# The first stage of a decoder step: pages of the cache in halves by two queues, x and w_ada asked for later, PSUM pools that wait by tile, and the last pair's compression sums without a pin

## The chip, the core and the metric

One core of a Trainium2 chip runs the whole program. Its engines are PE (TensorE, matrix products), DVE (VectorE), ACT (ScalarE), POOL (GpSimd) and SP (SyncE, which here only issues DMAs). Each engine works off its own queue of instructions in a fixed order; semaphores hold an instruction back until what it reads or overwrites is ready. DMAs are issued by SP, POOL and ACT, and an issue stands in the queue of its engine like any other instruction.

The metric is the device time in microseconds (us) of one execution, as the median of several runs.

## The reference, cut to what matters

One layer of a decoder runs over 512 prompt tokens and over 8 sampled sequences with 8 new tokens each and 2048 tokens in a paged cache. The part that matters here is the compression of the cached keys and values, and the normalization ahead of the first projection:

```python
def compress_blocks(x, pos, w1, w2):
    b, n = x.shape[:2]
    n_chunk = n // CMP_STRIDE
    xc = x[:, :n_chunk * CMP_STRIDE].reshape(b, n_chunk, CMP_STRIDE, NSA_GROUPS, HEAD_DIM)
    pos = pos.reshape(2, CMP_STRIDE, 1, HEAD_DIM)
    w1 = w1.reshape(2, CMP_STRIDE, HEAD_DIM, CMP_HIDDEN)
    lead = jnp.einsum('bncgd,cdh->bngh', xc + pos[0], w1[0])
    trail = jnp.einsum('bncgd,cdh->bngh', xc + pos[1], w1[1])
    return jnp.einsum('bngh,hd->bngd', jax.nn.silu(lead[:, :-1] + trail[:, 1:]), w2)
...
    mod = jnp.einsum('bd,de->be', jax.nn.silu(c), lp['w_ada']) + lp['b_ada']
    sh1, sc1, gt1, sh2, sc2, gt2 = jnp.split(mod[:, None, :], 6, axis=-1)
    h = rms_norm(x, lp['norm1_g']) * (1.0 + sc1) + sh1
    z = jnp.einsum('btd,dc->btc', h, lp['w_in'])
```

Everything after that (two attention branches, gates, output projection, MLP) is untouched.

## The kernel before

The program has stages: the first stage (`first_stage`, L542), the projection `z` in eight slabs (`step` in `run`, L2583, and `project`, L873), prompt attention, sample attention, the merge of the branches, and the MLP. Only the first stage and its seam with the projection are touched.

**Units.** The first stage compresses the pages of 8 sequences in 48 units (L578). Sequences 0 to 3 have 8 units each: four steps j, each once for keys (kv = 0) and once for values (kv = 1). Sequences 4 and 5 share 8 units, and 6 and 7 the last 8. Two sequences make a pair, and a pair adds up in three PSUM banks: `hid` for keys, `hid` for values, and one, `hids`, that both share. For every unit PE turns rows of a page (`ct` in the trace), ACT copies them out (`x`), DVE or, for the shared units, POOL makes their sums (`xs`), and PE multiplies them by the weights w1 (`hid`, then `hids`). The order on PE is: `ct` of unit u+1, `hid` and `hids` of unit u, then what the list `todo[u]` holds. `ro` is a copy on DVE that brings the page of a sequence (`cpg`, four buffers) into the order of the transposes.

**Sums.** When a pair is done, `cmp_act` (L503) reads its banks on ACT and DVE once for keys and once for values (in the trace `cst` and `csx`, and `r1w` for the last pair), and leaves silu of the sums; `cmp_out` multiplies that by w2. For pairs 0 to 2 it stands in `todo[14]`, `todo[15]` and so on; for pair 3 it comes after the loop, behind a pin (L678 to L681): its instructions go after the last split on DVE and the last high part on ACT. Keys and values use one buffer, `csx`, which the squares of the norms use too (`norm`, L556).

**Loads.** Pages are asked for by number, so a register is loaded for each; SP asks for half of sequence 0, half of 1, all of 2, then 4 to 7 when a buffer comes free; ACT asks for the other half of 0; POOL asks for the other half of 1 and all of 3 (L621), then w2, the tiles of `x` (three buffers), and eight tiles of `w_ada` (two buffers, 1 MB each), each waiting for the buffer it takes over. Late in that queue stand `late_loads` (L273): ptT, a copy of the page table, and four small constants. `stage_logf` (L696) turns ptT into row numbers (`lfrow`, on DVE) for a gather by POOL. Each DMA is pinned behind the one before it on its queue. `asked(f)` (L613) puts a small copy on POOL ahead of f, which waits for a sum xs.

**x and w_ada.** `norm(k)` takes the squares of x tile k on ACT, a reciprocal root in 13 small operations and a scaling on DVE; `turned(k)` transposes it on PE (`nt`) and copies it to `hf` (`adw` in the trace). `ada_first` (PE, `ada`) and its end make the modulation, and `modulate` applies it to `hf` on DVE.

**The seam.** At unit 46 `seam()` (L2537) opens the pools of the projection, splits the 8 rows of `hf` into high and low parts (`h`, ACT and DVE), and splits the first weights (`winh`, `winl`). The projection's matmuls need both. The first stage's banks come from the pool `psc`: three matmul banks, two for transposes, two for `hid`, one for `hids`. Then the pool `ps` takes the same eight banks (L2564). A pool waits, by default, for all of the pool before it; with `reuse_waits="tile"` a tile waits for the tiles whose place it takes. SBUF pools have that (L64), PSUM pools do not (L67).

**Order.** The order within each queue is made when the kernel is built, by a scheduler with a simulated time line; among what is ready it goes by the order in which the program is traced. On PE every matmul is chained behind the last one until the first slab of the projection is done, so there the written order holds. `issue_after` pins an instruction behind another one of the same engine.

## Time and profile before

| | |
|---|---|
| median of 3 runs | 1175.04 us (1172.7 to 1177.06) |
| the profiled execution | 1173.28 us, its span 1170.8 us |
| granted TensorE clock, mean | 0.992 |
| busy: PE, DVE, ACT, POOL | 96%, 67%, 48%, 26% |
| read from HBM, written | 217.64 MB, 57.12 MB |

Unit 0 starts on PE at 18.6 us of the span, unit 16 at 54.2, unit 32 at 93.7, unit 47 at 167.0, and the projection at 179.8. Times in the text are us from the start of the span. A row of the timeline gives start, duration, engine, line, operation, output and input with shapes, a count, and in brackets the idle time before it and what ended it. A row of the waits gives the engine, its operation and line, what released it, and then total us, number and longest. A row of the chain of waits gives start, duration, engine, output, line and count. A line number can be that of a helper (L83 is any matmul, L89 any transpose, L106 any tensor-tensor operation of DVE, L168 any DMA).

### The profile page before, as it was taken

What the parts mean: (1) busy time and instruction counts of PE and PEld (TensorE: products, weight loads), DVE (VectorE), ACT (ScalarE), POOL (GpSimd) and SP (SyncE); (2) the same over time, 40 slices, a digit from 0 to 9 for tenths busy, and PEclk for the clock granted to TensorE, in tenths of its full rate; (3) what the DMA queues carried; (4) which work ended last, traced back from release to release, by engine and by line L of the source; (5) the groups of instructions that cost most, each with busy time, mean ns of one, the idle gap of its engine ahead of it and who ended that gap; (6) DMA issues with size and microseconds to landing.
All of it is one profiled execution on the core that took longest, in us unless ns stands there. A gap on an engine that the chain in (4) does not pass through costs nothing.

```text
span 1170.8 us, 25266 instructions
## 1 busy us (share of the span) xinstructions
PE 1129.6 (96%) x9530; PEld 972.4 (83%) x9530; DVE 782.2 (67%) x1874; ACT 564.2 (48%) x1079; POOL 300.1 (26%) x353
## 2 busy tenths in 40 slices
PE   8897988999999998999999999999999999999998
PEld 5896768999865665777799999789999997888887
DVE  3566574668677897766656364768766754798676
ACT  1343352345576785555533222447565655565420
POOL 4314420000220111000576664010655411100000
PEclk9999998999999999999999999999999999999999
DMA  9998535587586559999899997337444537977732
GB/s 231 230 248 228 164 104 192 166 297 257 162 295 216 158 193 314 296 308 305 242 274 299 318 279 252 117 114 235 148 146 154 182 109 251 312 258 250 240 104 81
DMA packets 188187, 255.51 MB, mean 218 GB/s; under 512 B 23161, under 2 KB 144706, under 8 KB 185890
## 3 DMA queue, kind: packets, MB, share of 16 engines
q1 hardware_dynamic: 148770, 173.03, 47.9%
q0 software_dynamic: 21296, 67.38, 17.8%
q10 hardware_dynamic: 18000, 13.50, 4.0%
q8 instruction: 75, 1.23, 0.4%
q14 instruction: 46, 0.38, 0.1%
HBM read 217.64 MB, written 57.12 MB: 235 GB/s over the span
## 4 chain that ended last, share of the span: by engine, by line
PE 83%; DVE 8%; DMA 5%; issue 1%; ACT 1%; SPq 1%; POOL 0%; ACTq 0%; DVEq 0%
PE dn L83 14%; PE z L83 10%; PE mg L83 9%; PE br L83 4%; PE wo L83 4%; PE up L83 3%; DMA cpg<-in_cache_nsa_kv 3%; PE hid L83 3%; PE k L89 2%; PE ss L83 2%; PE so L83 2%; PE dns L83 2%; PE ct L89 2%; PE ada L83 2%; PE hids L83 2%
## 5 line engine op out<-in xcount | busy, mean ns | idle before, releaser
L83 PE MATMUL z<-winh,h 128*128 128x264 f32 (+1 forms) x576 | 111.5, 288 | 10.0 <-DVE r1w L106 10.0
L83 PEld LDWEIGHTS z<-winh,h 128*128 128x128 f32 x576 | 92.6, 193 | 11.5 <-issue 10.9
L83 PE MATMUL z<-winl,h 128*128 128x264 f32 (+1 forms) x320 | 88.7, 286 | 0.0
L83 PE MATMUL mg<-hH,wmh 128*128 128x288 f32 x240 | 70.2, 294 | 0.0
L83 PE MATMUL mg<-hH,wml 128*128 128x288 f32 x240 | 70.1, 294 | 0.0
L83 PE MATMUL mg<-hL,wmh 128*128 128x288 f32 x240 | 68.0, 293 | 0.0
L118 ACT ACTIVATE x<-ct 128x512 f32<-128x512 f32 x64 | 36.4, 596 | 65.4 <-PE ct L89 63.0
L83 PE MATMUL hid<-x,w1raw 128*128 128x128 f32 (+1 forms) x384 | 65.1, 313 | 0.2 <-ACT x L118 0.2
L83 PEld LDWEIGHTS z<-winl,h 128*128 128x128 f32 x320 | 61.3, 192 | 0.1
L83 PEld LDWEIGHTS hid<-x,w1raw 128*128 128x128 f32 x384 | 55.1, 194 | 3.0 <-ACT x L118 0.5
L83 PE MATMUL hids<-xs,w1sum 128*128 128x128 f32 (+1 forms) x192 | 37.7, 320 | 10.2 <-DVE ntt L106 6.0
L137 DVE TENSOR_TENSOR wml<-wmr,wmh 128x1024 fp32r<-128x1024 f32 x14 | 21.2, 1511 | 36.4 <-ACT wmh L118 36.4
L83 PEld LDWEIGHTS mg<-hH,wmh 128*128 128x128 f32 x240 | 45.1, 188 | 0.1
L83 PEld LDWEIGHTS mg<-hH,wml 128*128 128x128 f32 x240 | 45.0, 187 | 0.0
L137 DVE TENSOR_TENSOR wp<-sums,wp 128x1024 fp32r<-128x1024 f32 x26 | 38.3, 1477 | 9.2 <-ACT wp L118 8.7
L83 PEld LDWEIGHTS mg<-hL,wmh 128*128 128x128 f32 x240 | 44.3, 188 | 0.0
L137 DVE TENSOR_TENSOR wp<-pu,wp 128x512 fp32r<-128x512 f32 (+1 forms) x26 | 28.9, 1116 | 18.7 <-ACT wp L118 18.7
L83 PEld LDWEIGHTS hids<-xs,w1sum 128*128 128x128 f32 x192 | 29.9, 197 | 12.8 <-issue 8.6
L2073 POOL TENSOR_TENSOR td<-td 128x512 f32<-128x512 f32 x24 | 34.3, 1429 | 21.0 <-DMA td<-in_w_down 20.9
L89 PE MATMUL ct<-identF,ro 128*128 128x128 f32 x256 | 36.8, 278 | 2.6 <-DVE ro L121 2.6
L2073 POOL TENSOR_TENSOR td<-td,td 128x512 f32<-128x512 f32 x24 | 34.3, 1430 | 14.8 <-DMA td<-in_w_down 14.1
L83 PE MATMUL br<-oH,wbl 128*128 128x288 f32 x128 | 37.8, 295 | 0.0
(1175 smaller groups left out, 3565.6 us busy)
## 6 DMA issues: line engine op xcount, KB each, us to landing
adw<-in_w_ada SPq DMA_DIRECT2D x16, 1024.0 KB
foxD<-in_cache_fox_kv SPq DMA_DIRECT2D x128, 128.0 KB
rows<-in_cache_nsa_kv SPq DMA_DIRECT2D x128, 128.0 KB
rows<-foxD SPq DMA_DIRECT2D x26, 512.0 KB
pu<-in_w_up SPq DMA_DIRECT2D x26, 512.0 KB
wdr<-in_w_down SPq DMA_DIRECT2D x26, 512.0 KB
cpg<-in_cache_nsa_kv SPq DMA_DIRECT2D x96, 128.0 KB
td<-in_w_down POOLq DMA_DIRECT2D x24, 512.0 KB, 6.5
```

Of the source, the lines that this page charges most:

```text
L83: ins = self.nc.tensor.matmul(out, a, b, start=start, stop=stop, skip_group_check=True)
L89: ins = self.nc.tensor.transpose(out, in_, self.identF[:n, :n])
L118: return self.nc.scalar.activation(out, in_, f, **kw)
L137: self.splits.append((eng or self.nc.vector).tensor_tensor(l, x, h.bitcast(F32), op=OP.subtract).ins)
L2073: self.nc.gpsimd.tensor_tensor(out, x, y, op=OP.subtract)
```

## The change

1. PSUM pools get `reuse_waits="tile"`.
2. Of sequences 1, 2 and 3, SP asks for the first half of the pages and POOL for the second, in the order 1, 2, 3.
3. `late_loads` goes from unit 31 to unit 20. The tiles of x are asked for at units 22, 23, 23, 32 and 34 (were 15, 16, 16, 23 and 27), the first two of w_ada at 25 and 27 (24 and 28), the other six one unit later.
4. The norms go to units 29, 31, 33, 34 and 36 (were 18, 22, 26, 30 and 33), the turns to 31, 33, 35, 36 and 38 (22, 26, 30, 33 and 35). `ada_first` goes one unit back for the first six (30, 32, ... 40), the last two stay at 41 and 43. The first two `modulate` go from units 36 and 37 to unit 39. The first `stage_logf` goes from 32 to 33.
5. `cmp_act` of pair 3 is traced in units 46 (keys) and 47 (values), without the pin. Its buffers lie in the tile of w1 (its unused fifth and taps whose last use is unit 46); the tile `r1w` that takes the place of w1 is made after the last pair's keys are out, inside the first slab of the projection.

```diff
     def banks(self, name, ctx, mm):
-        self.ps = ctx.enter_context(self.tc.tile_pool(name=name, bufs=1, space=bass.MemoryType.PSUM))
+        self.ps = ctx.enter_context(self.tc.tile_pool(name=name, bufs=1, space=bass.MemoryType.PSUM, reuse_waits="tile"))
...
-        r1 = self.keep.tile([P, 5 * D], F32, tag="r1", bufs=1, name="w1raw")
+        r1 = self.r1 = self.keep.tile([P, 5 * D], F32, tag="r1", bufs=1, name="w1raw")
...
-        r = self.r1[:, TOK:TOK + 1536].rearrange("p (n c) -> p n c", n=3) if i == 3 else None
-        xb, th = (r[:, 0], r[:, 1 + kv]) if i == 3 else (pl.tile([P, 512], F32, tag="csx", name=f"csx{i}{kv}"),
+        v = self.r1.rearrange("p (n c) -> p n c", c=512)
+        xb, th = (v[:, 8], v[:, 0 if kv else 9]) if i == 3 else (pl.tile([P, 512], F32, tag="csx", name=f"csx{i}{kv}"),
...
-            r = self.r1[:, TOK + 1536:TOK + 2048].rearrange("p (n g d) -> p n g d", n=2, d=64) if i == 3 else None
+            r = self.r1[:, 512:1024].rearrange("p (n g d) -> p n g d", n=2, d=64) if i == 3 else None
...
-        self.cmp_pages("sync", 1, slice(0, 8))
+        for b in (1, 2, 3):
+            self.cmp_pages("sync", b, slice(0, 8))
         self.late_constants()
         self.ada_start()
         self.constants()
-        self.cmp_pages("sync", 2)
...
-        for k, u in enumerate((22, 26, 30, 33, 35)):
-            todo[u - (4 if u < 32 else 3 if u == 33 else 2)] += [lambda k=k: norm(k)]
+        for k, u in enumerate((31, 33, 35, 36, 38)):
+            todo[u - 2] += [lambda k=k: norm(k)]
             todo[u] += [lambda k=k: turned(k)]
...
-        todo[0] += [asked(lambda: (self.cmp_pages("gpsimd", 1, slice(8, 16)), self.cmp_pages("gpsimd", 3)))]
+        todo[0] += [asked(lambda: [self.cmp_pages("gpsimd", b, slice(8, 16)) for b in (1, 2, 3)])]
...
-        todo[15] += [asked(load_x)]
-        todo[16] += [load_x, load_x]
-        todo[24] += [asked(wada(0))]
-        todo[23] += [load_x]
-        todo[27] += [load_x]
-        todo[28] += [asked(wada(1))]
-        todo[31] += [self.late_loads]
+        todo[22] += [asked(load_x)]
+        todo[23] += [load_x, load_x]
+        todo[25] += [asked(wada(0))]
+        todo[32] += [load_x]
+        todo[34] += [load_x]
+        todo[27] += [asked(wada(1))]
+        todo[20] += [self.late_loads]
...
-        for k, u in enumerate((29, 31, 33, 35, 37, 39, 41, 43)):
+        for k, u in enumerate((30, 32, 34, 36, 38, 40, 41, 43)):
...
-                todo[(30, 32, 34, 36, 38, 40)[k - 2]] += [wada(k)]
+                todo[(31, 33, 35, 37, 39, 41)[k - 2]] += [wada(k)]
             if k % 2:
-                todo[max(u + 2, 36)] += [lambda k=k: self.modulate(0, hf, range(k - 1, k + 1))]
+                todo[max(u + 2, 39)] += [lambda k=k: self.modulate(0, hf, range(k - 1, k + 1))]
...
-        for y, u in enumerate((32, 36)):
+        for y, u in enumerate((33, 36)):
...
-        self.r1 = self.keep.tile([P, 5 * D], F32, tag="r1", bufs=1, name="r1w")
-        with behind():
-            for kv in range(2):
-                self.cmp_act(pl, 3, kv)
+            if u >= 46:
+                self.cmp_act(pl, 3, u - 46)
...
-        self.zS = self.r1[:NS, 0:TOK]
+        def room():
+            self.r1 = keep.tile([P, 5 * D], F32, tag="r1", bufs=1, name="r1w")
+            self.zS = self.r1[:NS, 0:TOK]
...
-            step(0, between=[lambda: None] + [lambda kv=kv: self.cmp_out(None, 3, kv) for kv in range(2)] + [lambda: self.cmp_keys(3)])
+            step(0, between=[lambda: None] + [lambda kv=kv: self.cmp_out(None, 3, kv) for kv in range(2)] + [lambda: (self.cmp_keys(3), room())])
```

## The prediction

> **What bounds the kernel now.** I read the page's busy shares first, then the waits of PE (TensorE), then stretches of the span, and the timeline at each wait.

> ```profile
> PE 1129.6 (96%) x9530; PEld 972.4 (83%) x9530; DVE 782.2 (67%) x1874; ACT 564.2 (48%) x1079; POOL 300.1 (26%) x353
> ...
> PE z L83 <- DVE r1w L106: 10.0, 1, 10.0
> PE hids L83 <- DVE ntt L106: 6.0, 1, 6.0
> PE hids L83 <- DVE csx L106: 4.2, 3, 2.1
> ```

> PE is the bound, idle for 41 us of 1170.8. 20.2 of these are the three waits above (us in total, times, longest), and all lie in the first stage, which is what the change rewrites. Whatever is saved there moves everything behind it, since the later stages are PE work with little idle time of their own (325 to 440 us below: PE 110.94 of 115). Of each stretch the rows give its length and the busy time of PE, weight loads, DVE (VectorE), ACT (ScalarE) and POOL (GpSimd), then PE's granted clock, the share of the DMA engines' time, and GB/s.

> ```profile
> 17.00:90.00 73.00, 68.79 (x650) 66.88 (x651) 45.62 (x148) 30.65 (x55) 24.73 (x44) 0.98 0.97 244
> 83.30:110.00 26.70, 20.18 (x162) 16.48 (x161) 15.36 (x56) 10.52 (x20) 10.19 (x12) 0.94 0.99 258
> 110.00:120.00 10.00, 9.30 (x72) 7.72 (x70) 9.27 (x32) 2.99 (x7) 3.77 (x3) 1.00 0.33 107
> 110.00:140.60 30.60, 29.90 (x215) 24.97 (x214) 21.97 (x64) 11.21 (x23) 13.24 (x11) 1.00 0.52 161
> 169.80:180.00 10.20, 0.23 (x1) 0.27 (x2) 8.99 (x20) 4.35 (x8) 1.80 (x5) 0.64 0.87 278
> 325.00:440.00 115.00, 110.94 (x812) 70.96 (x812) 93.61 (x325) 84.39 (x230) 19.94 (x31) 1.00 0.66 214
> ```

> PE stands still almost wholly from 169.8 to 180, with its granted clock down to 0.64, and loses 6.5 us from 83.3 to 110.

> **Part 1, pages in halves.** Before, sequence 2 came by SP alone while POOL fetched sequence 3, which is used a whole sequence later.

> ```profile
> 20.65 4.87 POOL L168 DMA_DIRECT2D cpg<-in_cache_nsa_kv  x8 [0.96 <-issue]
> ...
> 30.34 2.05 POOL L168 DMA_DIRECT2D cpg<-in_cache_nsa_kv  x3 [0.48 <-DMA cpg<-in_cache_nsa_kv]
> ...
> DMA to landing us min/median/max: 4.1/7.0/9.7
> ...
> 49.21 1.90 DVE L121 COPY ro<-cpg 128x1024 f32<-128x1024 f32 x3 [0.92 <-DMA cpg<-in_cache_nsa_kv]
> ...
> 53.24 0.71 PE L83 MATMUL hids<-xs,w1sum 128*128 128x128 f32 x4 [1.60 <-DVE csx L106]
> ...
> 57.35 0.68 PE L83 MATMUL hids<-xs,w1sum 128*128 128x128 f32 x4 [2.06 <-DVE csx L106]
> ```

> The two POOL rows are the first and the last of its first 16 page requests, the last out by 32.4 us. Those 16 are now halves of sequences 1 and 2, so with the longest landing, 9.7 us, sequence 2 is there by 42 us, not 49.2. DVE then loses the 0.92 us ahead of its copy, and the whole row of copies and sums behind it, which PE's two waits follow, comes 0.9 us earlier. The waits themselves stay but for that: DVE works without a gap in between. From nothing to both waits (3.7 us), I take **0.9**: the copy's idle time is the only one that the pages explain. [...] The row from 17 to 90 agrees that the engines are full (0.97); what changes is whose bytes go first.

> **Part 2, the page-table load ahead of x and w_ada.** The 5 small loads with ptT now follow w2 in POOL's queue.

> ```profile
> 52.73 0.18 POOL L616 COPY warm<-xs 128x1 f32<-128x1 f32 x1 [10.28 <-DVE xs L483]
> ...
> 87.00 0.56 POOL L168 DMA_DIRECT2D ptT<-in_page_table  x1
> ...
> 97.04 0.21 DVE L112 TENSOR_SCALAR lfrow<-ptT 128x1 int32<-128x1 int32 x2 [4.94 <-DMA ptT<-in_page_table]
> ...
> 101.56 2.05 PE L83 MATMUL hids<-xs,w1sum 128*128 128x256 f32 x4 [5.98 <-DVE ntt L106]
> ...
> 106.70 1.03 PE L83 MATMUL hids<-xs,w1sum 128*128 128x256 f32 x4
> ```

> They fit into POOL's 10.28 us of idle time, so they cost nothing; ptT is there long before its use, and the 4.94 us in which lfrow held DVE's queue go. Behind lfrow stood the sums that PE's hids waits for. The stretch from 83.3 to 140.6 (unit 29 to unit 40) has 57.3 us with 50.1 of PE, so 7.2 idle; the same four hids also took 2.05 us against 1.03, at a lowered clock: 8.2 in all.

> Against it: the norms of x tiles 0 to 2 and the turns of tiles 0 and 1 move into this stretch.

> ```profile
> L106 DVE TENSOR_TENSOR ntt<-nrs x10: 146/152/162, 64.0 to 110.2; 128x1 f32<-128x1 f32 x8, 64x1 f32<-64x1 f32 x2
> ...
> L110 DVE TENSOR_SCALAR x<-x,nrs x5: 745/753/754, 65.7 to 113.2; 128x1024 f32<-128x1024 f32 x4, 64x1024 f32<-64x1024 f32 x1
> ...
> 70.60 0.87 PE nt L89 x8
> ...
> 88.68 0.68 DVE L121 COPY adw<-nt 128x512 f32<-128x512 f32 x1
> ```

> A norm is 13 small operations of 0.152 and a scaling of 0.753, 2.7 us; a turn is 0.87 of PE and leaves DVE one copy of 0.68. Three norms and two copies are 9.6. DVE had 15.36 + 21.97 = 37.3 in the stretch and gets 46.9. How densely can DVE be filled without PE waiting? Of the rows above the fullest long stretch is 325 to 440 us, 0.81; the fullest short one is 110 to 120, 0.93, with PE at 9.30. PE's own work there becomes 50.1 + 1.7 = 51.8. DVE at 0.93 needs 50.4 us, less than that: no new waits. At 0.81 it needs 57.9: 6.1 us of them. The new stretch is packed like the short one but is long like the other, so I take the middle, **3 us of new waits** (the modulates of units 36 and 37 now meet in unit 39, but stay inside the stretch). Part 2 nets 8.2 - 3 = **5.2**, from 2.1 to 8.2.

> Loads that move cost nothing if these hold:

> ```profile
> x<-in_x_prompt POOLq DMA_DIRECT2D x4, 512.0 KB, 4.6
> wada<-in_w_ada POOLq DMA_DIRECT2D x8, 1024.0 KB, 8.6
> ...
> 130.59 1.73 PE hid L83 x8
> ...
> 142.58 1.73 PE hid L83 x8
> ```

> The last two rows are units 38 and 41, so three units take 12 us. The last two w_ada tiles have three units between the buffer's release and their use (four before); 8.6 us fit. x tile 3 now stands in POOL's queue behind a w_ada tile that waits for unit 30; its norm comes two units, 8 us, after its request; 4.6 fit. POOL's sums xs of the pairs stand behind both, as they did.

> **Part 3, the seam at 170 us.** A PSUM pool that waits as a whole made z's first matmul wait until the last of the old banks was read, at 179.6.

> ```profile
> 168.76 1.03 PE L83 MATMUL hids<-xs,w1sum 128*128 128x256 f32 x4
> ...
> 171.49 2.42 DVE L137 TENSOR_TENSOR winl<-winr,winh 128x1056 fp32r<-128x1056 f32 x2
> 173.83 0.60 DVE L106 TENSOR_TENSOR r1w<-r1w,hid 128x192 f32<-128x192 f32 x3
> 174.34 0.46 DVE L115 SCALAR_TENSOR_TENSOR r1w<-r1w,cmpb,hid 128x256 f32<-128x256 f32 x1
> 174.73 1.24 DVE L137 TENSOR_TENSOR winl<-winr,winh 128x1056 fp32r<-128x1056 f32 x1
> 175.90 0.60 DVE L106 TENSOR_TENSOR r1w<-hids,r1w 128x256 f32<-128x256 f32 x1
> ...
> 179.00 0.61 DVE L106 TENSOR_TENSOR r1w<-hids,r1w 128x256 f32<-128x256 f32 x1
> ...
> 179.76 7.47 PE z L83 x48
> 188.07 2.96 PE z L83 x24
> ```

> With waits by tile, z's first bank (one of the matmul banks, not of the sums) is free at once, and z waits for its operands: the rows of h, and the second half of the first weights, split when the first of the two winl at 171.49 ends (172.7). But a new wait comes: the sums of the last pair's keys are now traced ahead of unit 47, and as in unit 15 (the hids row at 53.24) the hids matmuls of unit 47 must then wait until DVE has read the shared hids bank for the keys. Queued behind these four matmuls is all of z. If DVE does the splits first and the sums at once after them, the read ends at 172.7 + 0.60 + 0.46 + 0.60 = 174.4, hids ends at 175.4, and z starts there, 4.4 us earlier. The idle time is still over 5 us, so z's slow start (7.47 against 2 x 2.96, 1.55 us) stays. [...]

> Ends: with DVE taking the sums before the last splits, half of z's first tile (1.48) is done when they end at 174.4, so it ends at 175.9 at full clock, against 179.76 + 1.55 + 2.96 = 184.3: 8.4. With the next slab's splits ahead too, as at 174.73, the read ends at 176.5: 2.2. I take **4.4**, the order in which these rows stand.

> **Sum.** 0.9 + 5.2 + 4.4 = 10.5. The profiled run took 1173.28 (span 1170.8), so 1162.8; the median, 1175.04, is 1.8 higher: **1164.5**.

> **Rivals.** (a) All of it goes well: DVE at 0.93 and sums before splits, 0.9 + 8.2 + 8.4 = 17.5, 1157.5. For it: the 0.93 of 110 to 120; against: at the seam the rows stand in the other order. (b) DVE becomes the bound of the stretch and the seam gets its low end: 0.9 + 2.1 + 2.2 = 5.2, 1169.8. (c) The change does not do what it says at the seam, because z's first bank lies on one that the sums still read: part 3 pays nothing, 1168.9. The profile does not show which bank is whose. (d) Slower: each turn of x on PE waits for its norm, two units (8 us) after it.

> ```profile
> 86.90 1.05 ACT L118 ACTIVATE sq<-x 128x1024 bf16<-128x1024 f32 x1
> ...
> 101.86 0.75 DVE L110 TENSOR_SCALAR x<-x,nrs 128x1024 f32<-128x1024 f32 x1
> ```

> This norm took 15.7 us, ptT's 4.94 included; the squares also share one buffer with the pair's sums, which now alternate with them. From 10.1 us a norm on (five turns late by 2.1) the 10.5 are gone; at 15.7, three turns late by 7.7, the kernel ends at 1164.5 + 23.1 = 1187.6. Against it: half of the 15.7 is the wait for ptT and what it held up. (e) The halves bring nothing, because the engines are as full with one order as with the other and the copy still waits: 9.6, 1165.4.

> **How the numbers follow.** Forecast 0.46 (own range 1160 to 1168), (e) 0.10, (a) 0.19, (b) 0.13, (c) 0.06, (d) 0.06. A measurement of this kernel tells about 0.5%, 5.9 us, from no change. Faster: the forecast, (e), (a) and a third of (c), 0.77; same: (b), at 5.2, and the rest of (c), at 6.1, 0.17; slower: (d), 0.06. The range takes in (a) with the pages at their upper end (3.7 for 0.9), 1154.7, and (b) with no gain from the pages, 1170.7, with 2.3 more for the spread of the runs before (their highest is 2.0 over their median): 1173.

> **What would show it.** Right: no wait of lfrow for ptT; the copy at unit 16 not waiting for a page; z's wait replaced by one of unit 47's hids for DVE, of about 4 to 6 us; DVE above 0.8 between units 29 and 40, with a few waits of 1 to 2 us. Wrong: z still waiting for the last read of hids; long waits for nt or for w_ada; PE idle of the first stage unchanged.

## The result and the profile after

The changed kernel took 1168.9 us in the median of nine runs (1166.17 to 1172.18), the kernel before 1176.15 in nine runs beside them (1172.7 to 1181.29). The ratio is 0.9936 with a 95% interval of 0.9916 to 0.9956: some 7.5 us faster. The prediction was 10.5 us, 1164.5, with 1160 to 1168 as its own range. The profiled execution of the changed kernel took 1168.9 us with a span of 1167.0; that of before 1173.28 and 1170.8.

The page's line of busy shares, changed kernel:

```profile
PE 1130.7 (97%) x9530; PEld 973.0 (83%) x9530; DVE 779.4 (67%) x1874; ACT 564.5 (48%) x1079; POOL 299.5 (26%) x353
```

The work is the same; only idle time can have gone. PE's waits in the changed kernel (engine, operation, what released it; total us, times, longest):

```profile
PE hids L83 <- DVE w1raw L106: 7.7, 1, 7.7
PE hids L83 <- DVE csx L106: 3.1, 2, 1.8
PE nt L89 <- DVE x L110: 3.0, 1, 3.0
PE ct L89 <- DVE ro L121: 2.9, 2, 1.8
...
PE adat L89 <- DVE adw L121: 1.4, 1, 1.4
```

Two of the three waits that the prediction started from are gone: z for DVE (10.0) and hids behind ntt (6.0). Three have come: the last unit's hids for DVE, 7.7, a turn of x for its norm, 3.0, and adat, 1.4. The new 7.7 stands where the 10.0 was. PE's queue at the seam, changed kernel:

```profile
163.65 1.89 PE L83 MATMUL hid<-x,w1raw 128*128 128x256 f32 x8
173.26 2.04 PE L83 MATMUL hids<-xs,w1sum 128*128 128x256 f32 x4 [7.72 <-DVE w1raw L106]
174.74 1.00 PE L83 MATMUL z<-winh,h 128*128 128x264 f32 x2
```

and DVE's queue in the same time:

```profile
168.10 1.25 DVE L137 TENSOR_TENSOR winl<-winr,winh 128x1056 fp32r<-128x1056 f32 x1
169.27 0.60 DVE L106 TENSOR_TENSOR w1raw<-w1raw,hid 128x192 f32<-128x192 f32 x3
169.78 0.47 DVE L115 SCALAR_TENSOR_TENSOR w1raw<-w1raw,cmpb,hid 128x256 f32<-128x256 f32 x1
170.17 2.42 DVE L137 TENSOR_TENSOR winl<-winr,winh 128x1056 fp32r<-128x1056 f32 x2
172.51 0.60 DVE L106 TENSOR_TENSOR w1raw<-hids,w1raw 128x256 f32<-128x256 f32 x1
...
175.76 0.66 DVE L106 TENSOR_TENSOR w1raw<-hids,w1raw 128x256 f32<-128x256 f32 x1
```

The hids matmuls of unit 47 need the keys' half of the shared bank read first. That read, at 172.51, stands behind the two splits at 170.17, which belong to the next slab of the projection. z, queued behind hids on PE, starts at 174.74, a second before the values' read at 175.76: its bank is no longer tied to that one.

Stretches of the changed kernel (length; busy time of PE, weight loads, DVE, ACT, POOL; PE's granted clock; share of the DMA engines; GB/s):

```profile
53.30:60.20 6.90, 5.66 (x28) 5.39 (x27) 4.03 (x12) 1.82 (x3) 0.00 (x0) 0.51 0.56 156
...
82.40:136.10 53.70, 49.26 (x375) 41.78 (x374) 44.57 (x156) 26.08 (x50) 20.99 (x19) 1.00 0.87 234
165.50:174.70 9.20, 1.48 (x5) 1.20 (x5) 8.34 (x18) 4.68 (x7) 0.00 (x0) 0.71 0.87 271
```

The first row is read in the last section. The second is the stretch of units 29 to 40, 53.70 us now and 57.35 before. DVE fills 0.83 of it. The third is the seam, from the last `hid` to the first z: 9.20 now, 10.84 before. Set side by side by such marks, the two profiles differ so:

| from, to | before | after | difference |
|---|---|---|---|
| span's start, first `ct` of unit 0 | 17.30 | 16.60 | -0.7 |
| to unit 16's first `hid` | 36.93 | 36.65 | -0.3 |
| to unit 29's | 29.05 | 29.10 | +0.05, though two turns (1.74) moved out; a lowered clock took 1.8 (last section) |
| to the end of unit 40's `hid` | 57.35 | 53.70 | -3.65, with two turns more and one `ada` (0.83) less |
| to the end of unit 47's | 28.29 | 29.46 | +1.2, with that `ada` |
| to z's first matmul | 10.84 | 9.20 | -1.6 |
| z's first 48 | 7.47 | 6.83 | -0.6 |
| to the end of the span | 983.57 | 985.43 | +1.9 |

Up to z's first 48 matmuls the changed kernel is 5.7 us ahead in these two profiles; 1.9 of that goes in later stages, where the change only moves the making of `r1w`. That last stretch takes from 983.6 to 989.8 us in the twelve profiles of this record, so 1.9 is within its spread. The median of the runs, not this pair, gives the size of the gain.

### The profile page after: what moved, and what is told of

Read it like the earlier page. It is cut to its first block, busy times and chain, and to the rows that moved or that the text cites. A ratio compares the mean times of both kernels' runs of the same rounds, so it can differ in the third digit from the quotient of the medians.

```text
span 1167.0 us, 25279 instructions
## 1 busy us (share of the span) xinstructions
PE 1130.7 (97%) x9530; PEld 973.0 (83%) x9530; DVE 779.4 (67%) x1874; ACT 564.5 (48%) x1079; POOL 299.5 (26%) x353
## 3 DMA queue, kind: packets, MB, share of 16 engines
q8 instruction: 75, 1.23, 0.4%
## 4 chain that ended last, share of the span: by engine, by line
PE 83%; DVE 8%; issue 3%; DMA 3%; ACT 1%; POOL 1%; SPq 0%; POOLq 0%; DVEq 0%; ACTq 0%
PE dn L83 14%; PE z L83 9%; PE mg L83 9%; PE br L83 4%; PE wo L83 4%; PE up L83 3%; PE hid L83 3%; PE k L89 2%; PE ss L83 2%; PE dns L83 2%; PE so L83 2%; PE ct L89 2%; PE hids L83 2%; PE ada L83 2%; PE sp L89 1%
## 5 line engine op out<-in xcount | busy, mean ns | idle before, releaser
L83 PE MATMUL z<-winh,h 128*128 128x264 f32 (+1 forms) x576 | 111.0, 287 | 0.0
L83 PEld LDWEIGHTS z<-winh,h 128*128 128x128 f32 x576 | 92.1, 191 | 1.3 <-issue 0.6
L83 PE MATMUL z<-winl,h 128*128 128x264 f32 (+1 forms) x320 | 88.2, 284 | 0.0
L83 PE MATMUL mg<-hH,wmh 128*128 128x288 f32 x240 | 70.2, 294 | 0.0
L83 PE MATMUL mg<-hH,wml 128*128 128x288 f32 x240 | 70.1, 294 | 0.0
L118 ACT ACTIVATE x<-ct 128x512 f32<-128x512 f32 x64 | 36.4, 596 | 66.1 <-PE ct L89 62.4
L83 PE MATMUL mg<-hL,wmh 128*128 128x288 f32 x240 | 68.0, 293 | 0.0
L83 PE MATMUL hid<-x,w1raw 128*128 128x128 f32 (+1 forms) x384 | 65.9, 316 | 0.2 <-ACT x L118 0.2
L83 PEld LDWEIGHTS z<-winl,h 128*128 128x128 f32 x320 | 60.9, 190 | 0.0
L83 PEld LDWEIGHTS hid<-x,w1raw 128*128 128x128 f32 x384 | 55.8, 197 | 3.0 <-ACT x L118 0.5
L137 DVE TENSOR_TENSOR wml<-wmr,wmh 128x1024 fp32r<-128x1024 f32 x14 | 20.6, 1472 | 50.6 <-ACT wmh L118 50.6
L83 PE MATMUL hids<-xs,w1sum 128*128 128x128 f32 (+1 forms) x192 | 37.8, 321 | 10.8 <-DVE w1raw L106 7.7
L83 PEld LDWEIGHTS mg<-hH,wmh 128*128 128x128 f32 x240 | 45.1, 188 | 0.1
L83 PEld LDWEIGHTS mg<-hH,wml 128*128 128x128 f32 x240 | 45.0, 187 | 0.0
L83 PEld LDWEIGHTS mg<-hL,wmh 128*128 128x128 f32 x240 | 44.3, 188 | 0.0
L137 DVE TENSOR_TENSOR wp<-sums,wp 128x1024 fp32r<-128x1024 f32 x26 | 37.8, 1459 | 9.1 <-ACT wp L118 8.6
L137 DVE TENSOR_TENSOR wp<-pu,wp 128x512 fp32r<-128x512 f32 (+1 forms) x26 | 29.3, 1134 | 18.0 <-ACT wp L118 15.8
L83 PEld LDWEIGHTS hids<-xs,w1sum 128*128 128x128 f32 x192 | 30.0, 198 | 13.4 <-issue 9.6
L89 PE MATMUL ct<-identF,ro 128*128 128x128 f32 x256 | 36.6, 277 | 2.9 <-DVE ro L121 2.9
L118 ACT ACTIVATE mgt<-mg 128x288 f32<-128x288 f32 x32 | 12.6, 408 | 54.7 <-PE mg L83 49.6
L118 ACT ACTIVATE u<-u 128x1152 f32<-128x1152 f32 x29 | 33.6, 1160 | 8.7 <-DVE u L106 8.1
## 6 DMA issues: line engine op xcount, KB each, us to landing
adw<-in_w_ada SPq DMA_DIRECT2D x16, 1024.0 KB
rows<-foxD SPq DMA_DIRECT2D x26, 512.0 KB
pu<-in_w_up SPq DMA_DIRECT2D x26, 512.0 KB
wdr<-in_w_down SPq DMA_DIRECT2D x26, 512.0 KB
td<-in_w_down POOLq DMA_DIRECT2D x24, 512.0 KB, 6.0
```

The lines of the kernel that those rows point to most:

```text
L83: ins = self.nc.tensor.matmul(out, a, b, start=start, stop=stop, skip_group_check=True)
L89: ins = self.nc.tensor.transpose(out, in_, self.identF[:n, :n])
L118: return self.nc.scalar.activation(out, in_, f, **kw)
L137: self.splits.append((eng or self.nc.vector).tensor_tensor(l, x, h.bitcast(F32), op=OP.subtract).ins)
```

## The experiments

The theory after the result: the gain at the seam fell short because the last pair's sums are now traced ahead of unit 47, which makes `hids` wait for DVE; the waits by tile would have done better without that; and the page-table load gives what was predicted, with a loss where the norms are packed closer. The rivals: DVE's splits at the seam are the bound whatever the sums do; the page-table load isn't worth its 8 us; the halves of the pages matter more, or less, than 0.9. Ratios are to the kernel before, run on the same chip beside each, with 95% intervals.

| kernel | us | ratio |
|---|---|---|
| changed kernel | 1168.9 | 0.9936 (0.9916 to 0.9956) |
| e1, sums behind unit 47 | 1161.56 | 0.9869 (0.9845 to 0.9894) |
| e2, waits by tile alone | 1166.31 | 0.9916 (0.9896 to 0.9936) |
| e3, page-table load alone | 1168.64 | 0.9933 (0.9915 to 0.9952) |
| e4, changed kernel, pages as before | 1171.83 | 0.9959 (0.9941 to 0.9977) |
| e5, tile and page-table load | 1157.45 | 0.9847 (0.9833 to 0.9862) |
| e6, e5 and halves | 1160.25 | 0.9865 (0.985 to 0.9881) |
| e7, changed kernel, x and w_ada as before | 1165.28 | 0.9912 (0.9897 to 0.9927) |
| e8, changed kernel without waits by tile | 1171.01 | 0.9956 (0.9941 to 0.9971) |
| e9, e1 and norms two units earlier | 1161.87 | 0.9881 (0.986 to 0.9902) |
| e10, e5 and sums behind unit 47, no pin | 1159.29 | 0.9854 (0.9835 to 0.9874) |

**e1: the sums traced behind unit 47.** Against the changed kernel:

```diff
-            if u >= 46:
-                self.cmp_act(pl, 3, u - 46)
+        for kv in range(2):
+            self.cmp_act(pl, 3, kv)
```

> The changed kernel, but the sums of the last pair are both traced behind unit 47, in the same buffers and without a pin. Theory (the changed kernel's hids of unit 47 waits 7.7 us because the keys' sums are traced ahead of it and share its bank): that wait goes, z starts within 1 us of unit 47's end, waits some 2 us in its first tile for the last split of the first weights, and the first compression output on PE comes 6 to 7 us earlier than in the changed kernel; time about 1162, 14 us under before. Rival (DVE's queue holds PE up whatever the order, and the wait only moves to the last pair's output, which needs the same sums): the wait shows again before the compression outputs, time within 2 us of the changed kernel's 1169.

PE's queue at the seam in e1:

```profile
164.47 1.03 PE L83 MATMUL hids<-xs,w1sum 128*128 128x256 f32 x4
165.14 0.59 PE L83 MATMUL z<-winh,h 128*128 128x264 f32 x2
...
168.50 0.39 PE L83 MATMUL z<-winl,h 128*128 128x264 f32 x1 [1.33 <-DVE winl L137]
...
173.75 1.10 PE L83 MATMUL co<-w2rawk,w1raw 128*128 128x64 f32 x8 [0.87 <-DVE w1raw L115]
```

and DVE's:

```profile
169.27 2.42 DVE L137 TENSOR_TENSOR winl<-winr,winh 128x1056 fp32r<-128x1056 f32 x2
171.60 0.64 DVE L106 TENSOR_TENSOR w1raw<-hids,w1raw 128x256 f32<-128x256 f32 x1
```

DVE does the same things in the same order as in the changed kernel, the splits ahead of the read. But PE doesn't wait for the read any more: z follows unit 47 at once, and of the 7.7 remain 1.33 for the second half of the first weights and 0.87 where the sums are multiplied on. That is worth 0.9936 - 0.9869, some 7.9 us, from two lines of tracing order. The rival that DVE's splits bind falls.

**e2 and e3: one part alone.** Each is one line on the kernel before:

```diff
-        self.ps = ctx.enter_context(self.tc.tile_pool(name=name, bufs=1, space=bass.MemoryType.PSUM))
+        self.ps = ctx.enter_context(self.tc.tile_pool(name=name, bufs=1, space=bass.MemoryType.PSUM, reuse_waits="tile"))
```

> The kernel before with its PSUM pools waiting by tile, nothing else. Theory (z waited for the whole old pool, its own bank was long free): z starts at about 170 instead of 179.8, its first tile is held up to about 172.7 for the last split, and the outputs of the last pair come 8 to 9 us earlier; time about 1167, as fast as the whole change or faster. Rival (z's first bank lies on a bank of the sums): z still starts at about 179.8, time as before, 1176.

```diff
-        todo[31] += [self.late_loads]
+        todo[20] += [self.late_loads]
```

> The kernel before with the page-table load and its four neighbours asked for at unit 20 instead of 31, nothing else. Theory: lfrow no longer waits 4.94 us, the wait of unit 32's hids falls from 6.0 to about 1 us, its matmuls no longer run slowly after it; 5 to 7 us less, about 1170. Rival (DVE is as late without it, because of the norms in its queue): the 6.0 stays above 4, time within 2 us of before.

In e2, PE's queue at the seam (the pin keeps the sums behind the splits, and z doesn't mind):

```profile
171.94 1.03 PE L83 MATMUL hids<-xs,w1sum 128*128 128x256 f32 x4
172.62 0.59 PE L83 MATMUL z<-winh,h 128*128 128x264 f32 x2
...
175.98 0.39 PE L83 MATMUL z<-winl,h 128*128 128x264 f32 x1 [1.33 <-DVE winl L137]
```

It gains 0.0084, some 9.9 us: by the ratios more than the whole change of which it is one line, though the two intervals overlap. In e3 PE's waits are:

```profile
PE z L83 <- DVE r1w L106: 10.0, 1, 10.0
PE hids L83 <- DVE csx L106: 4.1, 4, 2.1
```

The wait behind ntt (6.0) is gone, the one of z is as before, and the gain is 0.0067, 7.9 us (5.6 to 10.0 by the interval): near the 8.2 of the prediction, and more than the 5 to 7 expected ahead of this run. So each of the two waits is worth about what it lasts, and the rival to the page-table load falls.

**e4 and e6: the halves,** taken out of the changed kernel and put into e5. The edit in e4 (e6 has it the other way round):

```diff
-        for b in (1, 2, 3):
-            self.cmp_pages("sync", b, slice(0, 8))
+        self.cmp_pages("sync", 1, slice(0, 8))
...
+        self.cmp_pages("sync", 2)
...
-        todo[0] += [asked(lambda: [self.cmp_pages("gpsimd", b, slice(8, 16)) for b in (1, 2, 3)])]
+        todo[0] += [asked(lambda: (self.cmp_pages("gpsimd", 1, slice(8, 16)), self.cmp_pages("gpsimd", 3)))]
```

> The changed kernel with the pages asked for as before: SP half of 1 and all of 2, POOL the other half of 1 and all of 3. Prediction's term: 0.9 us slower than the changed kernel, with a wait of about 0.9 us of the copy at unit 16 for a page. Rival (the halves bring nothing, or cost the 1.1 us wait that the changed kernel shows at sequence 1's first copy): the same or up to 1 us faster.

> The same two lines and the pages of sequences 1 to 3 in halves. Prediction's term: 0.9 us less than without the halves. From the pair of the changed kernel and its twin with the pages as before: 2.7 us less, of unknown origin. Rival: no difference, the 2.7 us are the clock's (a lowered clock around 55 us in one profile of each) and the spread of the runs.

With the halves out, the changed kernel is 2.7 us slower by the ratios; with them in, e5 is 2.1 us slower. The intervals overlap in both pairs, and the signs differ, so no gain is shown either way, and the 0.9 that was expected in both is not seen. The traces say more. From the first `ct` of unit 0 to the first `hid` of unit 16, the six profiles with halves take 36.3 to 38.1 us (mean 36.7), the six without 36.2 to 38.4 (mean 36.8). That is the stretch in which the halves were to give 0.9. Unit 0 itself starts earlier with the halves, at 16.2 in the mean against 16.9, so that unit 16 starts at 52.9 against 53.7; the two sets overlap, and no run here shows whether the halves do that.

**e5 and e10: the best of the parts.** e5 is the kernel before with the lines of e2 and e3 and nothing else. e10 adds change 5 to it, in e1's form:

```diff
-        self.r1 = self.keep.tile([P, 5 * D], F32, tag="r1", bufs=1, name="r1w")
-        with behind():
-            for kv in range(2):
-                self.cmp_act(pl, 3, kv)
+        for kv in range(2):
+            self.cmp_act(pl, 3, kv)
```

> The kernel before with two of the change's lines: PSUM pools wait by tile, and the page-table load with its neighbours goes to unit 20. Theory (the two gains lie at different places and add; the rest of the change costs more than it brings): unit 47 ends at about 162, z starts within 1 us of it, time about 1159, ratio 0.985. Rival (what is saved early is lost at the seam, because DVE, not PE, is late there): z still starts at about 170, ratio 0.990 or more.

> The kernel before with waits by tile in PSUM, the page-table load at unit 20, and the last pair's sums without their pin and in the buffers of w1, both traced behind unit 47. Theory (once z no longer waits for the sums, the pin costs only the 0.9 us that the first output waits): 0 to 1 us less than with the two lines alone, 1157. Rival (without the pin the sums come ahead of the last splits in DVE's queue and hold z up): up to 2.5 us more.

PE's longest waits in e5:

```profile
PE hids L83 <- DVE csx L106: 4.6, 4, 2.1
PE ct L89 <- DVE ro L121: 2.8, 2, 1.5
...
PE z L83 <- DVE winl L137: 1.6, 2, 1.3
```

None is longer than 2.3 us. e5 gains 0.0153, 18.0 us, the sum of e2 and e3 (17.8), and beats the kernel before and the changed kernel. e10 is within its interval: with waits by tile, taking the pin away and moving the buffers shows no difference, as long as the sums are traced behind unit 47. Neither the 0 to 1 us expected of e10 nor the loss of its rival shows. The 0.9 us that the first output waits isn't the pin's either: `co` waits 0.90 with it (e5) and 0.87 without (e10).

**e7 and e9: the times of x and w_ada.** e7 puts change 4 and the loads of x and w_ada back to the units of before, and keeps the rest of the changed kernel. e9 is e1 with three norms two units earlier:

```diff
-            todo[u - 2] += [lambda k=k: norm(k)]
+            todo[u - (4 if k < 3 else 2)] += [lambda k=k: norm(k)]
```

> The changed kernel with x, the norms, the turns, w_ada, modulate and the gather of logf at the units where they stood before; the page-table load stays at unit 20. Theory (moving them is what costs: a 3.0 us wait for a norm at unit 31 and a 1.4 us one at unit 35): unit 47 ends 3 to 4 us earlier than in the changed kernel, time about 1165.5, ratio 0.991. Rival (the move costs nothing or pays, since x no longer competes with the pages): 1169 or more.

> The kernel with the last pair's sums traced behind unit 47, and the norms of x tiles 0, 1 and 2 traced two units earlier (27, 29, 31), their turns where they are. Theory (the late norms cost because two units are too short for the chain of a norm in DVE's queue): the 3.0 us wait of the turn at unit 31 goes, 2 to 3 us less than with the sums behind unit 47 alone, about 1159, ratio 0.985. Rival (DVE is simply full between units 29 and 40): the wait comes back as waits of hids or of a later turn, time within 1 us of 1161.6.

e7 is 0.0024 faster than the changed kernel, 2.8 us, as expected, but the two intervals overlap, and its profile doesn't help: the one execution that was profiled is the slowest of its runs, with a wait of its own,

```profile
PE ada L83 <- DMA wada<-in_w_ada: 2.5, 1, 2.5
```

so its unit 47 ends where the changed kernel's does, not the 3 to 4 us earlier that were expected. What the move costs is read better from e1 and e10, which differ by changes 2 to 4 (but for the page-table load, which both have at unit 20). From the first `hid` of unit 16 to the end of unit 47's, e1 and then e10:

```profile
54.12:164.63 110.51, 104.01 (x805) 91.49 (x804) 77.30 (x250) 48.45 (x90) 34.65 (x34) 1.00 0.65 187
55.19:163.62 108.43, 104.09 (x805) 91.52 (x804) 75.84 (x252) 48.43 (x90) 37.14 (x36) 1.00 0.68 190
```

The same PE work at full clock takes 2.1 us longer in e1. Between units 29 and 40, where most of the packing lies, it isn't the halves: without them the stretch takes 53.75 us with the new times (e4) and 51.1 with the old ones (e3, e5, e10).

In e9 I expected the wait for the norm to go and the time with it. The wait went, the time didn't. PE in e9:

```profile
94.53 2.04 PE L83 MATMUL hids<-xs,w1sum 128*128 128x256 f32 x4 [4.18 <-DVE nti L112]
```

and DVE's queue just ahead of that:

```profile
91.80 1.27 DVE L115 SCALAR_TENSOR_TENSOR coef<-modT,chT 128x18 f32<-128x18 f32 x1
92.99 0.74 DVE L110 TENSOR_SCALAR x<-x,nrs 128x1024 f32<-128x1024 f32 x1
...
93.78 0.60 DVE L106 TENSOR_TENSOR csx<-hids,cst 128x256 f32<-128x256 f32 x1
```

The norm that is now in time is done ahead of the read of hids that PE needs next. DVE's queue has little slack here (17.42 us busy of the 20 from 78 to 98 us in e9): in these two orders a different one of PE's operations waits. The theory of e9 falls, its rival holds.

**e8: the changed kernel without waits by tile** (the line of e2 taken back).

> The changed kernel without waits by tile in its PSUM pools. Theory (in the changed kernel the waiting by tile hardly pays, since hids of unit 47 stands ahead of z and waits for the same queue of DVE): z waits on for the last read of hids, at about 176.5 instead of 174.7; 1.7 us slower than the changed kernel, about 1170.6. Rival (the pool's wait is the larger part of the seam as in the kernel before): 5 us or more slower.

PE in e8:

```profile
172.46 2.04 PE L83 MATMUL hids<-xs,w1sum 128*128 128x256 f32 x4 [7.73 <-DVE w1raw L106]
175.73 0.78 PE L83 MATMUL z<-winh,h 128*128 128x264 f32 x2 [1.23 <-DVE w1raw L106]
```

The 7.7 stays, and z then waits 1.23 more, for the values. So the line that is worth 9.9 us alone is worth 0.0020, 2.4 us, in the changed kernel, and even that within overlapping intervals: `hids` holds z up for nearly the whole time that the pool would have.

## Why the prediction was off: the terms one by one

**Part 2 came out in its sum; its two terms are less sure.** The page-table load was to give 8.2 and gives 7.9 in the runs (e3). In the profiles the stretch of units 29 to 40 falls from 57.35 to 51.1 (kernel before and e3), which is 6.2, and from 59.9 to 51.1 (e2 and e5), which is 8.8: in e2 the clock was halved for 10.2 us at the wait of `hids`, in the kernel before for 3.4. In e3 PE keeps 2.4 us of waits there, which the prediction put at nothing. The closer packing of norms and turns was to cost 3 us of new waits. e7 puts the cost at 2.8, within overlapping intervals; e1 and e10 put it at 2.1. In the stretch the changed kernel takes 53.7, 2.6 more than e3's 51.1. Of that, 0.9 is work that moved (two turns in, one `ada` out, which the prediction didn't count), so 1.7 are waits.

The stretch was to fall from 57.3 by 8.2, and to gain 3 of waits and 1.7 of turns: 53.8; it is 53.7. That it fits so closely is luck, since in these two profiles the gain and the cost were both taken too large. The middle between the two densities, 0.93 and 0.81, was to the point: DVE is at 0.83. But the prediction expected several waits of 1 to 2 us; there were two, of 3.0 and 1.4, and how the first came about is in the last section. `lfrow` now waits 0.52 for ptT, at 51.14 us (row below), not 4.94 at 97.

**Part 3 is the step that failed, in its size.** The prediction named the wait that would come, `hids` of unit 47 for the read of the shared bank, and what would be queued behind it. It took 4.4, for "DVE does the splits first and the sums at once after them". DVE did the splits of the next slab in between as well, the order that the prediction put down as its lower end, 2.2. Measured is 1.6 at z's start and 0.6 in z's first 48 matmuls, 2.2 together; the profiles of e4 and e7, which have the same seam, give 0.9 and 1.7. That z's slow start would stay whole behind a wait of over 5 us was the author's estimate: behind the 7.72 us of the changed kernel z's first 48 took 6.83 us, with the clock at 0.50 for the first 1.44 of them, where they took 7.47 before. The prediction took 4.4 as "the order in which these rows stand", but that is a misreading: in its rows the read of hids, at 175.90, stands behind both of the next slab's splits, the second of the two at 171.49 and the one at 174.73. The rows were evidence for the lower end. With the pin gone the scheduler was free to put the read first, but it went on as it had; why is open.

The larger fault is what the prediction did not work out: the waits by tile without the new wait. It priced them only together with change 5, and set the upper end at 8.4 with the sums ahead of the splits. Alone they give 9.9 (e2), because z then needs nothing from the sums at all. Change 5 gives most of that back; traced one unit later it does not (e1).

**Part 1: 0.9 was more than there is.** Three rows of the changed kernel's timeline:

```profile
31.83 0.63 PE L89 MATMUL ct<-identF,ro 128*128 128x128 f32 x4 [1.10 <-DVE ro L121]
...
47.42 1.96 DVE L121 COPY ro<-cpg 128x1024 f32<-128x1024 f32 x3 [0.34 <-DMA cpg<-in_cache_nsa_kv]
...
51.14 0.21 DVE L112 TENSOR_SCALAR lfrow<-ptT 128x1 int32<-128x1 int32 x2 [0.52 <-DMA ptT<-in_page_table]
```

The copy at unit 16 waits 0.34 for its pages, not 0.92, and starts 1.8 us earlier than before, the direction that was predicted. Yet, counted from unit 0's start, PE reaches unit 16 no earlier over twelve profiles (36.7 against 36.8). In the changed kernel unit 8, the first of sequence 1, waits 1.10 for its copy instead, which waited 2.48 for a page (0.21 before), and `lfrow` has come to stand among the sums of the first pair. The experiments are in keeping with rival (e), that the halves bring nothing, but can't tell it from 0.9.

**The sum.** 0 + 5.1 (7.9 - 2.8) + 2.2 = 7.3, beside 7.5 measured and 10.5 predicted: 2.2 of the difference is part 3, 0.9 part 1. The terms are known to 1 or 2 us, so that the sum fits to 0.2 is chance.

**The rivals.** (c) is refuted: z starts before the values' read. The measured 1168.9 is the very time that (c) gave, and 0.9 above the forecast's own range; that is a coincidence, since what (c) rests on did not happen. (d) did not come: one turn of five waited, once, for 3.0. (b) was right at the seam and too low for the stretch, and (a) too high in both. What no rival held is that a part of the change could work against another part: e5, two lines of the diff, is 0.0089 or 10.5 us faster than all of it, with intervals far apart. Of that, 7.9 is the place of the sums (e1). The rest, 2.6 between e1 and e5, is within overlapping intervals; the profiles of e1 and e10 show 2.1 of it between unit 16 and the end of unit 47, beside the closer norms and the later loads, which they don't tell apart.

## What to carry to other kernels

A wait that is relaxed (by tile, not by pool) pays only if nothing new is put in front of the same consumer: look for every bank that two accumulations share, and trace its readers behind its last writer, not one unit ahead (7.9 us here). Where the operations of an engine are reordered by a scheduler, price a new wait by the order that the trace of before shows, not by the order that the edit permits. A change of several parts is worth taking apart: here two of its lines did more than all of them.

## What the runs showed of the hardware

**A small operation of DVE that takes ten times as long.** The norm that made PE wait 3.0 us in the changed kernel, in rows of DVE, POOL and PE:

```profile
87.98 0.89 POOL L168 DMA_DIRECT2D wada<-in_w_ada  x1 [14.05 <-PE ct L89]
...
88.58 1.61 DVE L115 SCALAR_TENSOR_TENSOR nrs<-ntt,nrs 128x1 f32<-128x1 f32 x1
88.89 1.27 POOL L485 TENSOR_TENSOR xs<-x 128x512 f32<-128x512 f32 x1
...
91.08 0.16 DVE L115 SCALAR_TENSOR_TENSOR nrs<-ntt,nrs 128x1 f32<-128x1 f32 x1
91.28 0.75 DVE L110 TENSOR_SCALAR x<-x,nrs 128x1024 f32<-128x1024 f32 x1
...
92.09 1.09 PE L89 MATMUL nt<-identF,x 128*128 128x128 f32 x8 [3.00 <-DVE x L110]
```

The same operation, with two inputs of one element a row, takes 0.16 us by itself (91.08) and 1.61 beside a POOL sum, and both end at 90.2. Those 1.45 us are about half of PE's wait. In the same profile four more operations of DVE with two inputs, of 1 to 18 elements a row, start while a POOL sum runs, at 95.12, 104.57, 135.72 and 149.25: they take 1.23 to 1.26 us and end within 0.04 us of that sum. The `coef` in e9, 1.27 us from 91.80, runs beside another such sum, 1.70 us from 91.34. That the sum is what holds DVE up isn't shown: by these rows DVE's operation starts 0.3 us ahead of the sum, while POOL issues a load. A packed DVE queue should be priced with POOL's sums beside it.

```profile
49.88:53.30 3.42, 1.60 (x15) 1.41 (x14) 2.14 (x9) 1.41 (x3) 0.00 (x0) 1.00 0.61 177
49.77:53.18 3.41, 1.87 (x17) 1.68 (x16) 3.41 (x10) 1.54 (x3) 0.40 (x2) 1.00 0.48 132
```

The first was followed by half clock, the second wasn't. So it goes in all twelve: PE was busy for at most 2.05 us in each of the 35 windows at full clock that were followed by half clock, and for at least 1.43 us in each of the 3990 that were not; 39 of these were at 2.05 or less. In the profile of before the 2.06 us of wait are divided between two windows, of which the first has PE busy for 2.04 us, and the clock stays full. So in these traces the drop goes with how much of PE's waiting falls into one window, and that differs from execution to execution. No experiment here moved a wait against the windows, and what decides between 1.43 and 2.05 is open.

**The spread of the runs goes with this clock.** In the nine runs of the changed kernel the mean clock goes from 0.991 (1172.18 us) to 0.996 (1166.17), and the time falls by 1.16 us for each 0.001 that it rises, by a straight line through the nine. The five runs of e5 have 0.999 to 1.000 and lie between 1156.69 and 1159.46. A single profile can therefore be 3 us off the median for no reason of its order, and a gain of 1 us is not to be had from one.
